# Adding the halves of a narrow expert block on the way out of PSUM, in a decoder trunk with a mixture of experts

## Chip, cores and metric

The kernel runs on 1 core of one Trainium2 chip. The metric is the device time of one execution in microseconds (us); before the change the median of 3 runs is 1606.11 us (1605.93 to 1607.49).

## The reference

A two-layer decoder trunk on 256 tokens of width 1024. What matters here is the last sub-layer, a mixture of 8 SwiGLU experts of which each token takes two, with gates from a softmax over its two logits:

```python
def expert_block(args):
    xb, e = args
    gu = xb @ w13[e]                       # 1024 -> 2 x 3584
    return (jax.nn.silu(gu[:, :EXPERT_DIM]) * gu[:, EXPERT_DIM:]) @ w2[e]
```

Everything is float32. The weights of all eight experts, 8 x 44 MB, are read from HBM once.

## The kernel before

**Precision.** A float32 operand is split in two parts: hi is ScalarE's copy into TensorE's reduced type (L77), lo is what VectorE's subtraction leaves (L78). A product takes three matmuls, hi x hi, hi x lo, lo x hi (`mm3`, L306 to L309).

**Weights.** `Stream` (L35 to L89) loads 1 MB at a time on SyncE's queue (L59) into a handful of raw buffers, and splits each load in two pieces. A split is emitted when the ring `parts` has a free place out of five (N_PARTS, L31), so the split of a piece stands four pieces ahead of its use. A raw buffer is reused when its second piece is subtracted.

**Blocks.** Experts are ordered by their number of tokens ("places" 0 to 7). A wide block holds 128 tokens. A narrow block holds 64, and its gathered input `xs` carries the hi parts in columns 0 to 63 and the lo parts in 64 to 127; so two matmuls with `xs` as the stationary side (L1186, L1187) do the work of three, and the result has the sum split over two halves of partitions: rows 0 to 63 and rows 64 to 127 of PSUM have to be added. Places 0, 2, 3, 4 have a wide block, place 1 a wide and a narrow one, places 5, 6, 7 a narrow one each: four narrow blocks.

**Stages.** An expert is done in slices of 512 of its 3584 hidden columns (j = 0 to 6, L155): stage g (gate projection), stage u (up projection), and, one slice later, stage w (down projection of slice j - 1). A stage takes four pieces. The order of all stages is written out by hand (L163 to L188): places 0, 2, 3 in a chain, then the 21 stages of place 1, each followed by three stages of the chain 7, 6, 5, then place 4. `run_stage` (L1254) projects and takes the result out of PSUM. In stage g a wide block's result goes through Silu on ScalarE (L1297); a narrow block's is copied by ScalarE (L1300). In stage u the wide block's is multiplied in by VectorE (L1303); the narrow block's is copied by ScalarE (L1306), and `hidden` is queued.

**Small steps in between.** `beat_` (L1131), called after each piece, takes one step of the generator at the head of `quick` and, every second time, one of `slow` (gathers, finishing a block). For a narrow block `hidden` (L1189) waits one beat, then in two beats adds the halves of g and of u and transposes them at once, by a matmul of 128 rows of `gs` or `us` against `fold`, two 64 x 64 identities below each other (L1207); Silu (L1209) and the product (L1211) follow on the transposed values, and in a fourth beat the split into hi and lo (L1215, L1216) which stage w takes. A wide block waits three beats, then does four transposes (L1197) and the split.

**Order.** The engines run what is emitted in order. The PSUM pool `mm` has four banks, taken in turn (`bank`, L108).

Of the kernel before, what the change touches and what calls it, by code (L numbers as in the profile page):

```python
# [10 lines left out]
F32 = mybir.dt.float32  # L11
# [3 lines left out]
AF = mybir.ActivationFunctionType  # L15
# [77 lines left out]
def trunk(ctx, tc, x, mem, a_w_in, a_conv_w, a_conv_b, a_w_rgate, a_b_rgate, a_w_igate, a_b_igate,  # L93
# [3 lines left out]
    PE, ACT, DVE, POOL, SP = nc.tensor, nc.scalar, nc.vector, nc.gpsimd, nc.sync  # L97
# [10 lines left out]
    def bank():  # L108
        return psum.tile([128, 512], F32, name="mm")
# [161 lines left out]
    ident = const.tile([128, 128], F32, name="ident")  # L271
# [39 lines left out]
    def w_piece(a_hi, a_lo):  # L311

        p = bank().rearrange("p (m c) -> p m c", m=2)
        for m in range(2):
            w_hi, w_lo = st.get()
            for k in range(KT):
                mm3(p[:, m], w_hi[:, k], w_lo[:, k], a_hi[:, k], a_lo[:, k], k == 0, k == KT - 1)
            if m == 0:
                tick()
        return p  # L320
# [311 lines left out]
    for i in range(4):  # L632
        p = w_piece(x_hi, x_lo)
# [5 lines left out]
    for i in range(2):  # L639
        p = w_piece(x_hi, x_lo)  # L640
# [4 lines left out]
    for i in range(2):  # L645
        p = w_piece(mem_hi, mem_lo)
# [4 lines left out]
    p = t_pieces(mem_hi, mem_lo, 2)  # L651
# [31 lines left out]
    for t in range(2):  # L683
        p = w_piece(mem_hi, mem_lo)
# [45 lines left out]
    p = t_pieces(mem_hi, mem_lo)  # L730
# [161 lines left out]
    for i in range(2):  # L892
        p = w_piece(x_hi, x_lo)
# [3 lines left out]
    for i in range(4):  # L897
        p = w_piece(x_hi, x_lo)
# [4 lines left out]
    for i in range(4):  # L903
        p = w_piece(x_hi, x_lo)
# [6 lines left out]
    for c in range(2):  # L911
        p = t_pieces(x_hi, x_lo)
# [27 lines left out]
    for t in range(2):  # L940
        for h in range(2):
            p = bank().rearrange("p (k c) -> p k c", k=4)
# [13 lines left out]
    mo = ctx.enter_context(tc.tile_pool(name="mo", bufs=1))  # L956
# [3 lines left out]
    def mt():  # L960

        if "mt" not in late:
            assert not any(slot in early for _, slot in st.loaded) and not any(slot in early for slot in st.free)
            ep.close()
            late["mt"] = ctx.enter_context(tc.tile_pool(name="mt", bufs=2))
        return late["mt"]
# [16 lines left out]
    for r in range(2):  # L983
        mr = S(f"m{r}", 2)
        DVE.tensor_reduce(mr, l, axis=AX.X, op=OP.max)
        c = S(f"c{r}", 2, 8)
# [36 lines left out]

    ord_i = mo.tile([1, NE - 1], I32, name="ord_i")
    cs_i = mo.tile([1, NE + 1], I32, name="cs_i")
    fold = mo.tile([128, 64], F32, name="fold")
    y = h3

    h3_parts = []
# [1 line left out]
    def plan():  # L1031

        d = S("d", 2)
        POOL.tensor_sub(d, m[1], m[0])
        ACT.activation(d, d, AF.Exp)
        yield
        cnt = S("cnt", 8)
        DVE.tensor_copy(cnt, ct[:, 16:24])
        POOL.tensor_copy(rank[:, :, 0:1], val[:, :, 0:1])
        q = NE - 1  # L1040
        e7 = slots[:, 1:NE]
        key = S("key", q)
        DVE.scalar_tensor_tensor(key, cnt[:, 1:], 8.0, e7, op0=OP.mult, op1=OP.subtract)
        cmp = S("cmp", q, q)
        DVE.tensor_tensor(cmp, key[:, None, :].to_broadcast([128, q, q]), key[:, :, None].to_broadcast([128, q, q]),
                          op=OP.is_gt)
        yield
        pos = S("pos", q)
        DVE.tensor_reduce(pos, cmp, axis=AX.X, op=OP.add)
        sel = S("sel", q, q)  # L1050
        DVE.tensor_tensor(sel, pos[:, None, :].to_broadcast([128, q, q]),
                          slots[:, 0:q, None].to_broadcast([128, q, q]), op=OP.is_equal)
        yield
        ordr = S("ordr", q)
        POOL.tensor_mul(cmp, sel, e7[:, None, :].to_broadcast([128, q, q]))
        DVE.tensor_reduce(ordr, cmp, axis=AX.X, op=OP.add)
        POOL.tensor_copy(ord_i, ordr[0:1])
        yield
        tmp = S("tmp", 2, q, q)
        for t in range(2):  # L1060
            POOL.tensor_tensor(tmp[:, t], sel, val[:, t, None, 1:].to_broadcast([128, q, q]), op=OP.mult)
        DVE.tensor_reduce(rank[:, :, 1:], tmp, axis=AX.X, op=OP.add)
        yield
        for bs in PLACE.values():
            for b in bs:
                if b[0]:
                    dispatch(b)
            if bs[0][0] % 2:
                yield
        g1 = S("g1", 2)  # L1070
        POOL.tensor_scalar(g1, d, 1.0, None, op0=OP.add)
        DVE.reciprocal(g1, g1)
        POOL.tensor_mul(d, d, g1)
        yield
        ge = S("ge", 2, 8)
        POOL.tensor_tensor(ge, oh[0], bc(g1), op=OP.mult)
        POOL.tensor_tensor(oh[1], oh[1], bc(d), op=OP.mult)
        POOL.tensor_add(ge, ge, oh[1])
        yield
        POOL.tensor_copy(gate[:, :, 0:1], ge[:, :, 0:1])  # L1080
        for t in range(2):
            POOL.tensor_tensor(tmp[:, t], sel, ge[:, t, None, 1:].to_broadcast([128, q, q]), op=OP.mult)
        DVE.tensor_reduce(gate[:, :, 1:], tmp, axis=AX.X, op=OP.add)
        yield
        cs = S("cs", NE)
        POOL.tensor_copy(cs[:, 0:1], cnt[:, 0:1])
        POOL.tensor_mul(cmp, sel, cnt[:, None, 1:].to_broadcast([128, q, q]))
        DVE.tensor_reduce(cs[:, 1:], cmp, axis=AX.X, op=OP.add)
        yield
        room = S("room", NE)  # L1090
        for p in range(NE):
            POOL.memset(room[:, p:p + 1], float(sum(b[2] for b in PLACE[p])))
        POOL.tensor_sub(cs, cs, room)
        over = S("over", 1)
        DVE.tensor_reduce(over, cs, axis=AX.X, op=OP.max)
        yield
        DVE.tensor_scalar(over, over, 0.0, None, op0=OP.max)
        DVE.tensor_scalar(cs, cs, 0.0, None, op0=OP.max)
        POOL.tensor_copy(cs_i[:, :NE], cs[0:1])
        POOL.tensor_copy(cs_i[:, NE:], over[0:1])  # L1100
        yield
        POOL.tensor_add(fold, ident[:, 0:64], ident[:, 64:128])
        h3_parts.extend(hp.tile([128, 2, D], F32R, name=f"h3_{s}") for s in ("hi", "lo"))
        hi, lo = h3_parts
        for t in range(2):
            ACT.activation(hi[:, t], h3[:, t], AF.Copy)
            DVE.tensor_sub(lo[:, t], h3[:, t], hi[:, t].bitcast(F32))
            yield
        for t in range(2):
            ACT.activation(y[:, t], h3[:, t], AF.Copy, scale=ALPHA)  # L1110
            yield
# [65 lines left out]
    def project(o, b, w, kts, w_hi, w_lo, first, last):  # L1177

        for i, kt in enumerate(kts):
            a, z = first and i == 0, last and i == len(kts) - 1  # L1180
            for h in range(len(o)):
# [3 lines left out]
                else:  # L1185
                    PE.matmul(o[h], lhsT=w[:, kt], rhs=w_hi[:, i, f], start=a, stop=False)  # L1186
                    PE.matmul(o[h], lhsT=w[:, kt], rhs=w_lo[:, i, f], start=False, stop=z)  # L1187

    def hidden(b, j):  # L1189

        yield
        if b.wide:
            yield
            yield
            p = bank().rearrange("p (i c) -> p i c", i=4)
            for i in range(4):
                PE.transpose(p[:, i], b.sg[:, i * 128:(i + 1) * 128], ident)  # L1197
            hd = [mt().tile([128, 4, 128], F32R, name="hs", bufs=4) if (b.place, j) == (4, NJ - 1) else
                  mw.tile([128, 4, 128], F32R, name=f"hd_{s}") for s in ("hi", "lo")]
            hi, lo = hd  # L1200
        else:
            h = mt().tile([128, 4, 64], F32, name="sh")
            for src in (b.gs, b.us):

                p = bank()[:, :256].rearrange("p (i c) -> p i c", i=4)
                for i in range(4):
                    PE.matmul(p[:, i], lhsT=src[:, i * 128:(i + 1) * 128], rhs=fold, start=True, stop=True)  # L1207
                if src is b.gs:
                    ACT.activation(h, p, AF.Silu)  # L1209
                else:  # L1210
                    DVE.tensor_mul(h, h, p)  # L1211
                yield
            hd = mt().tile([128, 4, 128], F32R, name="hs", bufs=4)
            hi, lo, p = hd[:, :, 0:64], hd[:, :, 64:], h
        ACT.activation(hi, p, AF.Copy)  # L1215
        DVE.tensor_sub(lo, p, hi.bitcast(F32))  # L1216
        b.h[j] = hd
# [36 lines left out]
    def run_stage(blocks, kind, j, s):  # L1254
# [38 lines left out]
        for b, p in zip(blocks, o):  # L1293
            if kind == "g":
                if b.wide:
                    b.sg = mw.tile([128, 512], F32, name="sg")
                    ACT.activation(b.sg, p, AF.Silu)  # L1297
                else:
                    b.gs = mt().tile([128, 512], F32, name="gs")
                    ACT.activation(b.gs, p, AF.Copy)  # L1300
            else:
                if b.wide:
                    DVE.tensor_mul(b.sg, b.sg, p)  # L1303
                else:
                    b.us = mt().tile([128, 512], F32, name="us")
                    ACT.activation(b.us, p, AF.Copy)  # L1306

                quick.append(hidden(b, j))

    def run_experts(seq, blocks, s, hooks):  # L1310
# [75 lines left out]
    with tc.If(more > 0):  # L1386
        for p in (0, 1, 2, 3, 5, 6, 7):
            c = nc.values_load(cs_i[0:1, p:p + 1], min_val=0, max_val=2 * T,
                               skip_runtime_bounds_check_because="a count of at most 256 tokens")
            with tc.If(c > 0):  # L1390
# [3 lines left out]
                b = Block(key)  # L1394
# [78 lines left out]
```

## Time and profile before

| | |
|---|---|
| median of 3 runs | 1606.11 us (1605.93 to 1607.49) |
| the profiled execution | 1606.54 us |
| its span, first to last instruction | 1604.8 us |
| TensorE's mean granted clock | 0.996 |
| loaded from HBM | 449.00 MB |

The expert layer starts near 557 us. The first narrow stage's result leaves PSUM at 959.4 us (L1300), the last narrow hidden step ends near 1454 us (L1216). How to read the rows: a group gives line, engine, operation, output <- inputs, form, count, then busy us and mean ns of one, then the engine's idle time just before them and what ended it. A time-line row gives the start in us, the length in us, engine, line, operation, output <- inputs, form and count, and in brackets the idle time of the engine before it and what ended that. Matmuls are pipelined, so that their lengths overlap; the time that one holds the engine is the distance between starts.

### The profile page before, as it was taken

To read this page: it belongs to the slowest core of one execution; us is meant where nothing else is said; L and a number is where in the kernel's file an instruction comes from. 1 tells how busy PE (TensorE), PEld (TensorE's weight loads), DVE (VectorE), ACT (ScalarE), POOL (GpSimd) and SP (SyncE) were. 2 spreads that over 40 slices of the span, in tenths; PEclk is the share of its full clock that TensorE was granted. 3 is DMA by queue.
4 is the path that set the end of the run, shared out by engine and by line. 5 is a ranking of instruction groups with operands and counts; after the bars stand their busy time and mean duration, and the time that the engine had idled before them with its cause. 6 is when DMAs were issued, how large, how long until landed. Compare 5 with 4: busy or idle time off the path is not lost.

```text
span 1604.8 us, 23215 instructions
## 1 busy us (share of the span) xinstructions
PE 1582.8 (99%) x8585; PEld 1340.6 (84%) x8585; DVE 1263.1 (79%) x1464; ACT 1091.9 (68%) x1419; POOL 37.1 (2%) x60
## 2 busy tenths in 40 slices
PE   8999999999999999999999999999999999999996
PEld 7988999998998877888888888888888888888775
DVE  6678545546657689888988879888798889789976
ACT  5784544443546368787787778778778777778774
POOL 0000000000000113000000000000000000000000
PEclk9999999999999999999999999999999999999998
DMA  9454655556443789999996999999999999999991
GB/s 290 158 190 151 237 185 185 184 187 205 135 133 135 272 302 352 356 357 332 360 364 224 352 309 341 355 357 370 326 354 359 362 365 345 336 362 359 342 321 47
DMA packets 218682, 451.63 MB, mean 281 GB/s; under 512 B 7241, under 2 KB 62610, under 8 KB 218562
## 3 DMA queue, kind: packets, MB, share of 16 engines
q1 hardware_dynamic: 217490, 446.76, 78.5%
q0 software_dynamic: 1072, 3.32, 0.7%
q8 instruction: 69, 1.13, 0.3%
q14 instruction: 51, 0.42, 0.1%
HBM read 449.00 MB, written 1.05 MB: 280 GB/s over the span
## 4 chain that ended last, share of the span: by engine, by line
PE 93%; DVE 3%; ACT 2%; issue 1%; DMA 1%; POOL 0%; POOLq 0%; SPq 0%; ACTq 0%
PE mm L307 14%; PE mm L309 14%; PE mm L308 14%; PE mm L1186 7%; PE mm L1187 7%; PE acc L307 7%; PE acc L308 7%; PE acc L309 7%; PE mm L1207 3%; PE acc L1186 3%; PE acc L1187 2%; DVE w_lo L78 2%; PE mm L1170 1%; PE mm L1197 1%; ACT w_hi L77 1%
## 5 line engine op out<-in xcount | busy, mean ns | idle before, releaser
L78 DVE TENSOR_TENSOR w_lo<-raw,w_hi 128x1024 fp32r<-128x1024 f32 x509 | 610.1, 1223 | 188.3 <-ACT w_hi L77 184.8
L77 ACT ACTIVATE w_hi<-raw 128x1024 fp32r<-128x1024 f32 x509 | 525.3, 1056 | 141.4 <-PE mm L308 42.8
L307 PE MATMUL mm<-w_hi,xg_hi 128*128 128x512 f32 x560 | 225.2, 402 | 0.2 <-ACT w_hi L77 0.2
L307 PE MATMUL mm<-x_hi,w_hi 128*128 128x256 f32 x768 | 220.4, 287 | 2.4 <-ACT w_hi L77 2.4
L308 PE MATMUL mm<-w_lo,xg_hi 128*128 128x512 f32 x560 | 221.4, 395 | 1.2 <-DVE w_lo L78 1.2
L309 PE MATMUL mm<-w_hi,xg_lo 128*128 128x512 f32 x560 | 221.3, 395 | 0.0
L309 PE MATMUL mm<-x_hi,w_lo 128*128 128x256 f32 x768 | 218.6, 285 | 1.1 <-DVE w_lo L78 1.1
L308 PE MATMUL mm<-x_lo,w_hi 128*128 128x256 f32 x768 | 218.0, 284 | 0.0
L1186 PE MATMUL mm<-w_hi,xs 128*128 128x512 f32 x448 | 179.0, 400 | 0.0
L1187 PE MATMUL mm<-w_lo,xs 128*128 128x512 f32 x448 | 176.9, 395 | 0.0
L307 PEld LDWEIGHTS mm<-x_hi,w_hi 128*128 128x128 f32 x768 | 148.0, 193 | 5.6 <-ACT w_hi L77 2.9
L309 PEld LDWEIGHTS mm<-x_hi,w_lo 128*128 128x128 f32 x768 | 148.0, 193 | 1.7 <-DVE w_lo L78 1.6
L308 PEld LDWEIGHTS mm<-x_lo,w_hi 128*128 128x128 f32 x768 | 148.0, 193 | 0.6
L307 PEld LDWEIGHTS mm<-w_hi,xg_hi 128*128 128x128 f32 x560 | 105.3, 188 | 25.7 <-ACT xs L1352 1.5
L309 PEld LDWEIGHTS mm<-w_hi,xg_lo 128*128 128x128 f32 x560 | 105.1, 188 | 25.2
L308 PEld LDWEIGHTS mm<-w_lo,xg_hi 128*128 128x128 f32 x560 | 105.4, 188 | 24.9 <-DVE w_lo L78 2.2
L78 DVE TENSOR_TENSOR w_lo<-x_hi,w_hi 128x1024 fp32r<-128x1024 f32 x86 | 103.7, 1223 | 15.3 <-ACT w_hi L77 15.2
L78 DVE TENSOR_TENSOR w_lo<-x_lo,w_hi 128x1024 fp32r<-128x1024 f32 x86 | 103.4, 1222 | 13.4 <-ACT w_hi L77 13.2
L78 DVE TENSOR_TENSOR w_lo<-h,w_hi 128x1024 fp32r<-128x1024 f32 x84 | 100.9, 1222 | 14.4 <-ACT w_hi L77 14.0
L307 PE MATMUL acc<-w_hi,hd_hi 128*128 128x512 f32 x272 | 108.1, 398 | 0.0
L308 PE MATMUL acc<-w_lo,hd_hi 128*128 128x512 f32 x272 | 107.4, 395 | 0.0
L309 PE MATMUL acc<-w_hi,hd_lo 128*128 128x512 f32 x272 | 107.4, 395 | 0.0
(379 smaller groups left out, 2645.6 us busy)
## 6 DMA issues: line engine op xcount, KB each, us to landing
raw<-in_moe_w SPq DMA_DIRECT2D x169, 1024.0 KB, 5.5
x_hi<-in_moe_w SPq DMA_DIRECT2D x43, 1024.0 KB, 5.4
x_lo<-in_moe_w SPq DMA_DIRECT2D x43, 1024.0 KB, 6.2
raw<-in_ffn_w SPq DMA_DIRECT2D x42, 1024.0 KB, 5.0
h<-in_moe_w SPq DMA_DIRECT2D x42, 1024.0 KB, 5.5
e<-in_moe_w SPq DMA_DIRECT2D x36, 1024.0 KB, 5.9
raw<-in_a_w_in SPq DMA_DIRECT2D x10, 1024.0 KB, 9.5
raw<-in_mem_w_kv SPq DMA_DIRECT2D x8, 1024.0 KB
```

What stands on the lines that cost most here:

```text
L77: nc.scalar.activation(hi, src, AF.Copy)
L78: nc.vector.tensor_sub(lo, src, hi.bitcast(F32))
L307: PE.matmul(o, lhsT=l_hi, rhs=r_hi, start=start, stop=False)
L308: PE.matmul(o, lhsT=l_hi, rhs=r_lo, start=False, stop=False)
L309: PE.matmul(o, lhsT=l_lo, rhs=r_hi, start=False, stop=stop)
L1170: PE.matmul(p[:, k], lhsT=src[:, t, f], rhs=disp[:, t, g0:g0 + ng], start=t == 0, stop=t == 1)
L1186: PE.matmul(o[h], lhsT=w[:, kt], rhs=w_hi[:, i, f], start=a, stop=False)
L1187: PE.matmul(o[h], lhsT=w[:, kt], rhs=w_lo[:, i, f], start=False, stop=z)
L1197: PE.transpose(p[:, i], b.sg[:, i * 128:(i + 1) * 128], ident)
L1207: PE.matmul(p[:, i], lhsT=src[:, i * 128:(i + 1) * 128], rhs=fold, start=True, stop=True)
```

## The change

The halves are now added as they leave PSUM. ScalarE copies rows 64 to 127 into rows 0 to 63 of an SBUF tile, and VectorE adds rows 0 to 63 from PSUM. In stage g, Silu follows on ScalarE; in stage u, the product on VectorE. `hidden` waits three beats for a narrow block as for a wide one, and transposes the product alone, with four transposes of 64 rows; the split then reads PSUM. The tile `fold` goes.

```diff
-    fold = mo.tile([128, 64], F32, name="fold")
...
-        POOL.tensor_add(fold, ident[:, 0:64], ident[:, 64:128])
...
+    def halves_sum(p, name):
+
+        a = mt().tile([64, 512], F32, name=name)
+        ACT.activation(a, p[64:128], AF.Copy)
+        DVE.tensor_add(a, a, p[0:64])
+        return a
+
     def hidden(b, j):
 
         yield
+        yield
+        yield
+        n, src = (128, b.sg) if b.wide else (64, b.us)
+        p = bank()[:, :4 * n].rearrange("p (i c) -> p i c", i=4)
+        for i in range(4):
+            PE.transpose(p[:, i], src[:, i * 128:(i + 1) * 128], ident[:n, :n])
         if b.wide:
-            yield
-            yield
-            p = bank().rearrange("p (i c) -> p i c", i=4)
-            for i in range(4):
-                PE.transpose(p[:, i], b.sg[:, i * 128:(i + 1) * 128], ident)
...
         else:
-            h = mt().tile([128, 4, 64], F32, name="sh")
-            for src in (b.gs, b.us):
-
-                p = bank()[:, :256].rearrange("p (i c) -> p i c", i=4)
-                for i in range(4):
-                    PE.matmul(p[:, i], lhsT=src[:, i * 128:(i + 1) * 128], rhs=fold, start=True, stop=True)
-                if src is b.gs:
-                    ACT.activation(h, p, AF.Silu)
-                else:
-                    DVE.tensor_mul(h, h, p)
-                yield
             hd = mt().tile([128, 4, 128], F32R, name="hs", bufs=4)
-            hi, lo, p = hd[:, :, 0:64], hd[:, :, 64:], h
+            hi, lo = hd[:, :, 0:64], hd[:, :, 64:]
         ACT.activation(hi, p, AF.Copy)
         DVE.tensor_sub(lo, p, hi.bitcast(F32))
...
                 else:
-                    b.gs = mt().tile([128, 512], F32, name="gs")
-                    ACT.activation(b.gs, p, AF.Copy)
+                    b.gs = halves_sum(p, "gs")
+                    ACT.activation(b.gs, b.gs, AF.Silu)
             else:
...
                 else:
-                    b.us = mt().tile([128, 512], F32, name="us")
-                    ACT.activation(b.us, p, AF.Copy)
-
+                    b.us = halves_sum(p, "us")
+                    DVE.tensor_mul(b.us, b.us, b.gs)
                 quick.append(hidden(b, j))
```

## Rows read from the trace of the kernel before

**Rows 1.** The page, part 1: busy us (share of the span) and instructions.
```profile
PE 1582.8 (99%) x8585; PEld 1340.6 (84%) x8585; DVE 1263.1 (79%) x1464; ACT 1091.9 (68%) x1419; POOL 37.1 (2%) x60
```
**Rows 2.** Windows, 953 to 1453: PE, PEld, DVE, ACT, POOL, clock, DMA share, GB/s.
```profile
953.00:1453.00 500.00, 500.00 (x2440) 413.52 (x2439) 435.37 (x436) 394.14 (x499) 2.09 (x4) 1.00 0.97 351
```
**Rows 3.** Time-line of TensorE, 1051 to 1084.
```profile
1066.35 1.00 PE L1207 MATMUL mm<-fold,gs 128*128 128x64 f32 x8
1067.16 0.48 PE L1186 MATMUL acc<-w_hi,hs 128*128 128x512 f32 x1
...
1073.74 0.40 PE L307 MATMUL mm<-w_hi,xg_hi 128*128 128x512 f32 x1
...
1083.07 0.40 PE L1186 MATMUL mm<-w_hi,xs 128*128 128x512 f32 x1
```
**Rows 4.** Time-line of VectorE, 1060 to 1085.
```profile
1070.50 0.42 DVE L1211 TENSOR_TENSOR sh<-sh,mm 128x256 f32<-128x256 f32 x1
...
1072.35 6.91 DVE L78 TENSOR_TENSOR w_lo<-raw,w_hi 128x1024 fp32r<-128x1024 f32 x6
...
1084.85 1.23 DVE L78 TENSOR_TENSOR w_lo<-h,w_hi 128x1024 fp32r<-128x1024 f32 x1 [1.82 <-ACT w_hi L77]
```
**Rows 5.** Time-line of ScalarE, 1061 to 1086.
```profile
1070.95 0.42 ACT L1215 ACTIVATE hs<-sh 128x256 fp32r<-128x256 f32 x1 [1.05 <-DVE sh L1211]
...
1080.71 1.06 ACT L77 ACTIVATE w_hi<-raw 128x1024 fp32r<-128x1024 f32 x1 [1.27 <-DVE w_lo L78]
...
1083.27 0.60 ACT L1300 ACTIVATE gs<-mm 128x512 f32<-128x512 f32 x1 [0.33 <-PE mm L1187]
```
**Rows 6.** Windows, L1207 alone, 953 to 1453: PE, PEld, clock, DMA share, GB/s.
```profile
953.00:1453.00 500.00, 55.99 (x448) 58.65 (x448) 1.00 0.97 351
```
**Rows 7.** Time-line of TensorE around a wide block's four transposes.
```profile
590.81 0.60 PE L1197 MATMUL mm<-ident,sg 128*128 128x128 f32 x4
591.16 0.48 PE L307 MATMUL mm<-w_hi,xg_hi 128*128 128x512 f32 x1
591.48 0.39 PE L308 MATMUL mm<-w_lo,xg_hi 128*128 128x512 f32 x1
591.71 0.40 PE L309 MATMUL mm<-w_hi,xg_lo 128*128 128x512 f32 x1
```
**Rows 8.** Groups of VectorE, 953 to 1453.
```profile
L78 DVE TENSOR_TENSOR w_lo<-raw,w_hi 128x1024 fp32r<-128x1024 f32 x191 | 226.3, 1222 | 41.4 <-ACT w_hi L77 39.3 <-PE mm L1186 1.8
...
L1211 DVE TENSOR_TENSOR sh<-sh,mm 128x256 f32<-128x256 f32 x28 | 11.7, 416 | 0.0
...
L1281 DVE TENSOR_TENSOR ys<-ys,mm 128x512 f32<-128x512 f32 x12 | 7.7, 681 | 0.0
L1243 DVE TENSOR_TENSOR y_lo<-ys,y_hi 128x512 fp32r<-128x512 f32 x7 | 4.8, 686 | 0.0
```
**Rows 9.** Groups of ScalarE, 953 to 1453.
```profile
L1215 ACT ACTIVATE hs<-sh 128x256 fp32r<-128x256 f32 x28 | 11.7, 418 | 24.9 <-DVE sh L1211 24.9
...
L1242 ACT ACTIVATE y_hi<-ys 128x512 fp32r<-128x512 f32 x7 | 4.4, 622 | 0.0
```
**Rows 10.** Windows, L78 alone, 953 to 1453: DVE, clock, DMA share, GB/s.
```profile
953.00:1453.00 500.00, 394.08 (x335) 1.00 0.97 351
```
**Rows 11.** Time-line of VectorE ahead of two other long stages.
```profile
1116.43 2.44 DVE L78 TENSOR_TENSOR w_lo<-raw,w_hi 128x1024 fp32r<-128x1024 f32 x2
...
1216.51 2.36 DVE L78 TENSOR_TENSOR w_lo<-x_lo,w_hi 128x1024 fp32r<-128x1024 f32 x2
```
**Rows 12.** Time-line of TensorE: first matmul of these two long stages.
```profile
1120.61 0.40 PE L307 MATMUL acc<-w_hi,hd_hi 128*128 128x512 f32 x1
...
1218.51 0.40 PE L307 MATMUL mm<-w_hi,xg_hi 128*128 128x512 f32 x1
```
**Rows 13.** DMA, 953 to 1453: GB/s in 40 equal slices.
```profile
GB/s 258 398 345 317 352 349 380 354 339 354 367 370 386 364 334 346 279 364 321 374 338 361 374 385 367 346 366 345 368 327 335 354 382 353 374 273 390 321 371 353
```

## The prediction

> **What bounds the kernel now.** The page comes first: TensorE is busy 99% of the span, VectorE 79%, ScalarE 68% [rows 1]. That is an average over stages, so the stretch that holds all narrow blocks is read next, 953 to 1453 us [rows 2]: TensorE 500.0 of 500 us, VectorE 435.4, ScalarE 394.1, the DMA engines at 0.97, the granted clock 1.00. The time-line then says how full TensorE really is. One period is a long stage (the wide and the narrow block of place 1 together, four split pieces at 2.33 us) and the three short stages behind it (u, w, g of one narrow block of places 5 to 7). TensorE runs through it without a gap. But the long stage starts at 1073.74 [rows 3], and the subtraction that made its first piece (counted off in the order of use) started at 1072.35 and, at 1.22 us, ended at 1073.57 [rows 4]: 0.17 us to spare. So two engines bound this stretch in turn: TensorE the long stages, in which ScalarE waits 1.27 us for a place in the ring of five pieces and VectorE then 1.82 us for ScalarE [rows 4, 5], and VectorE, just not late, the short ones.
>
> One rule differs here. TensorE's matmuls fill all 500 us, its weight loads 413.5, VectorE 435.4 [rows 2]. The Trainium skill (Perfetto Trace Analysis, Identifying the Most-Contended Engine) says that matmul busy time is a bad measure of headroom and that weight-load share, and occupancy for the other engines, are the good ones. By that rule VectorE would be the bound already and all that is added to it would count, an estimate of 41 to 90 us by the terms below. The trace agrees only in part, since its matmuls follow one another without a gap: the sum lets VectorE's idle time be eaten first.
>
> **What goes from TensorE.** Per narrow block and slice of 512 hidden columns, 28 times: eight fold matmuls, 16 records [rows 6]. Eight records hold the next matmul back from 1066.35 to 1067.16, 0.81 us [rows 3]; behind a group of transposes the first matmul takes 0.32 us to the next start against 0.23 [rows 7], and I charge the folds the same 0.09. So 1.8 us a slice. Four transposes come back. The wide block's four cost 0.35 + 0.09 = 0.44 us [rows 7]; with half the columns perhaps half. I take 0.44, the only row; the other end is 0.2. Net 1.36 us (to 1.6), in all 38 us (to 45) of TensorE time. The fold tile's one addition on GpSimd goes too; that engine is busy 2% [rows 1], and I cost it at nothing; it would still be under a microsecond if nothing covered it.
>
> **What comes to VectorE.** Gone: the product sh out of PSUM, 0.416 us [rows 8]. The subtraction behind it stays, of the same size, now from PSUM. New: two additions of 64 x 512 (SBUF and PSUM) and one product of 64 x 512. No row has 64 partitions. A row's time follows its columns (256: 0.416, 512: 0.681, 1024: 1.222 [rows 8]), so I take the 128 x 512 rows, 0.68 for SBUF with PSUM and 0.69 for SBUF alone; half of that, 0.34, is the low end, and no row speaks for more. In a queue each overlaps its follower by 0.09 (six subtractions take 6.91 us, 1.135 apart [rows 4]). The net is 28 x (3 x 0.60 - 0.33) = 41 us queued, 28 x (3 x 0.68 - 0.416) = 45 us alone, 13 us at the low end.
>
> **What comes to ScalarE.** Two copies and a Silu of 512 columns and a split copy, against two copies, a Silu of 256 and a split copy: some 0.2 us a slice more, 6 us. I cost it at nothing; its cover is the engine's 106 us of idle time [rows 2], and without that it is those 6 us.
>
> **The added wait.** In stage g the Silu stands right behind the copy in ScalarE's order and needs VectorE's addition; the next weight split stands behind the Silu. So VectorE first runs its queue empty up to the addition. Then it has nothing to do until Silu (0.62 for an SBUF-to-SBUF pass of 512 columns [rows 9], 0.1 of it beside its follower) and the next split copy (1.06 [rows 5]) are done. A hop costs 0.03: sh ended at 1070.92, its reader on ScalarE started at 1070.95 [rows 4, 5]. That makes a hole of 0.03 + 0.52 + 1.06 + 0.03, about 1.6 us, in VectorE per slice; 28 are 45 us. ScalarE's present wait for sh, 24.9 us in all [rows 9], goes, but no wait of TensorE hangs on it now, so it gives nothing back. Stage u adds no hole: addition and product stand behind each other on VectorE while ScalarE goes on splitting. SyncE issues a load when a subtraction frees its buffer, so its queue moves with VectorE; no load is moved past another.
>
> **The sum over the stretch.** VectorE needs 435 + 41 (or 45) + 45 = 521 to 525 us. Its lone subtractions close up if it never idles: 394.1 us for 335 [rows 10] is 1.176 each, queued 1.135, 14 us less. So 507 to 525 us against 500: 7 to 25 us longer, while TensorE's own need falls to 462.
>
> **The same, step by step,** for the period at 1073.74. The long stage's four subtractions end at 1072.35 + 3 x 1.135 + 1.22 = 1076.98. Addition, Silu and split copy follow, so the next subtraction starts at 1079.2 instead of 1076.9, and four of them end at 1083.8, 0.7 after the long stage ends (1083.07 [rows 3]).
> After a long g, place 1's narrow half has the same hole: its copy ends at 1083.87 [rows 5], addition, Silu and split copy end near 1086.2, and the next subtraction starts there instead of at 1084.85 [rows 4], 1.35 late. Addition and product (1.2) for one product (0.33) add 0.87; 0.17 was to spare: 2.0 us longer.
> After a long w the two additions into ys stand there as before: 0.75 late, 0.87 more. To spare were 1218.51 less the end of the subtraction begun at 1216.51, 0.78 [rows 11, 12]: 0.85 longer.
> After a long u: 0.7 late, 0.87 more. TensorE had four folds more there, so 1120.61 less the end of the pair begun at 1116.43, 1.74, was to spare [rows 11, 12]: 0.15 shorter.
> Three periods cost 2.7 us, seven rounds 19. Periods that also hold a block's finish or a gather have more to spare and may give back 5. Both ways meet near **16 us**. The profiled execution took 1606.54 us (span 1604.8, 1.7 around it), 0.4 above the median of the runs, so the forecast is 1606 + 16 = **1622 us**.
>
> **Rivals.** (1) TensorE stays the bound and the change is *faster*: 38 us, 1568 us. Place: the hole in stage g. With VectorE's closed-up work at 435 + 41 - 14 = 462 us it decides at (500 - 462) / 28 = 1.36 us a slice; each 0.1 us below that gives 2.8 us. For it: TensorE's 500 of 500, and that an addition on half the partitions, if it took half the time, would take 28 us off the sum, to 1594. Against: nothing can overtake a Silu and a split copy on ScalarE, and the long stage's slack is already spent in the walk. Loads don't cap it: the stretch ran at 351 GB/s [rows 2], with slices of 12.5 us at 398 [rows 13], at which its 175 MB take 441 us. The Trainium skill (Perfetto Trace Analysis, Roofline) gives 358 GB/s as a core's share and about 435 as a lone core's ceiling. By the first only some 10 us could be gained, by the second all 38; the slices above 358 speak for the second. Chance 0.15, from 1568 to 1602.
> (2) Hole and slack cancel, 1606 us: chance 0.08.
> (3) *Much slower*: a PSUM bank was free when ScalarE had copied it; now VectorE's addition frees it, up to three subtractions (3.4 us) later. Four banks rotate, so a bank is wanted again four allocations on. If TensorE waits 1 us for one in each slice, that is 28 us more, 1650 us. Against: four allocations are more than one short stage (3.7 us), and the new hidden step takes one bank where the old one took two. Chance 0.1.
> (4) The change doesn't do what it says: the folds are there, 448 records [rows 6], so this can only be the half-time additions, counted under (1).
>
> **Chances.** VectorE late by work and holes has 0.67; its own range is 1613 to 1631 (7 and 25 us). Within 0.2% (3 us, about what a measurement of this kernel can tell from no change) 0.08; faster 0.15; slower 0.67 + 0.1 = 0.77. To leave out no more than 2 in 10 the range reaches down to 1602, with most of rival 1 outside, and up to 1642, with most of rival 3 outside.
>
> **What would show it.** In the same stretch: VectorE over 92% busy; TensorE with gaps ended by w_lo, at the start of long stages and in the short ones; ScalarE idle ahead of Silu in stage g, ended by VectorE's addition, 28 times 1 to 3 us; VectorE idle some 1.6 us behind that addition, ended by ScalarE's split; additions and products near 0.68 us; transposes near 0.35 us per four. If TensorE has no gap, rival 1 is right and the forecast wrong; if its gaps are ended by a bank's reader, rival 3; if the additions take 0.34 us, the size is wrong.

## The result: slower by 26 us, and the profile after

The median after the change is 1632.67 us (1631.59 to 1634.18, four runs) against 1606.3 for the kernel before in the same session. The ratio is 1.0164, 95% interval 1.0146 to 1.0181. The forecast was 1622 us, range 1602 to 1642, slower with a chance of 0.77. Sign and mechanism came as forecast; the size is 26 us where 16 were forecast. The profiled execution took 1631.59 us, its span is 1629.5, so the two profiled executions differ by 25.05 us.

The page of the kernel after, its busy times (part 1) and the engines of its chain of waits (part 4):

```profile
PE 1578.6 (97%) x8249; PEld 1287.9 (79%) x8249; DVE 1299.6 (80%) x1520; ACT 1102.4 (68%) x1419; POOL 33.3 (2%) x59
...
PE 80%; DVE 12%; ACT 4%; issue 3%; DMA 1%; DVEq 0%; POOLq 0%; POOL 0%; SPq 0%; ACTq 0%
```

Beside [rows 1] TensorE has 336 matmuls fewer (28 slices, each with sixteen records of folds less and four transposes more), and its busy time has hardly fallen. A matmul that waits for its weights may be drawn long (0.50 us for 0.39 in the rows of TensorE below), so busy time hides part of the wait. The chain tells more: of the span, TensorE carries 80% (93% before) and VectorE 12% (3% before).

In what follows *the stretch* runs from the first matmul of place 1 to the first of place 4. It was 949.74 to 1451.64 us before, 501.9 us, and is 949.76 to 1474.31 after, 524.5: 22.6 us of the 25. The windows of the stretch, of before and then of after (columns: PE, PEld, DVE, ACT, POOL, clock, DMA share, GB/s):

```profile
949.00:1452.00 503.00, 503.00 (x2455) 415.98 (x2454) 437.83 (x438) 396.12 (x500) 2.09 (x4) 1.00 0.97 351
```
```profile
949.00:1474.00 525.00, 497.24 (x2114) 362.75 (x2113) 472.10 (x492) 405.43 (x500) 0.64 (x1) 1.00 0.93 335
```

VectorE has 34.3 us more to do and is idle for 52.9 us. The waits of the same stretch of after (engine, what waited, for what; us in all, times, longest):

```profile
ACT gs L1295 <- DVE gs L1191: 82.6, 28, 5.1
DVE w_lo L78 <- ACT w_hi L77: 50.1, 35, 1.6
PEld mm L1185 <- DVE w_lo L78: 36.8, 62, 2.0
PEld acc L1185 <- DVE w_lo L78: 19.4, 45, 1.1
...
PE mm L1185 <- DVE w_lo L78: 13.7, 22, 1.6
...
PE mm L1202 <- DVE us L1301: 5.0, 13, 0.5
...
PE mm L1184 <- DVE h L1227: 1.5, 1, 1.5
```

This is a ring of waits. ScalarE's Silu (L1295) waits 28 times for VectorE's addition, 2.95 us each. VectorE then waits for ScalarE's split, and nearly all of its idle time is that (50.1 of 52.9). TensorE's matmuls and weight loads wait for `w_lo`, and hardly for anything else: no wait for a bank's reader is of any size. One round of it in the time-lines of VectorE, ScalarE and TensorE (a long stage starts at 1081.91):

```profile
1081.32 4.61 DVE L78 TENSOR_TENSOR w_lo<-raw,w_hi 128x1024 fp32r<-128x1024 f32 x4
1085.86 0.67 DVE L1191 TENSOR_TENSOR gs<-gs,mm 64x512 f32<-64x512 f32 x1
1088.18 4.63 DVE L78 TENSOR_TENSOR w_lo<-raw,w_hi 128x1024 fp32r<-128x1024 f32 x4 [1.65 <-ACT w_hi L77]
1092.73 0.67 DVE L1191 TENSOR_TENSOR gs<-gs,mm 64x512 f32<-64x512 f32 x1
1095.05 2.36 DVE L78 TENSOR_TENSOR w_lo<-h,w_hi 128x1024 fp32r<-128x1024 f32 x2 [1.65 <-ACT w_hi L77]
```
```profile
1082.11 0.59 ACT L1190 ACTIVATE gs<-mm 64x512 f32<-64x512 f32 x1
1086.56 0.63 ACT L1295 ACTIVATE gs<-gs 64x512 f32<-64x512 f32 x1 [3.86 <-DVE gs L1191]
1087.10 3.89 ACT L77 ACTIVATE w_hi<-raw 128x1024 fp32r<-128x1024 f32 x4
```
```profile
1081.91 0.39 PE L307 MATMUL mm<-w_hi,xg_hi 128*128 128x512 f32 x1
1082.58 0.50 PE L308 MATMUL mm<-w_lo,xg_hi 128*128 128x512 f32 x1 [0.28 <-DVE w_lo L78]
...
1095.51 0.39 PE L1184 MATMUL acc<-w_hi,hs 128*128 128x512 f32 x1
1096.33 0.50 PE L1185 MATMUL acc<-w_lo,hs 128*128 128x512 f32 x1 [0.42 <-DVE w_lo L78]
```

The copy of the upper half is done at 1082.70, but the addition stands behind four queued subtractions and starts at 1085.86. Silu follows at 1086.56, the split at 1087.10, and the next subtraction at 1088.18: VectorE stood still for 1.65 us, and then again 7 us later. TensorE's next matmul with the lo part comes 0.67 and 0.82 us behind the one ahead of it, where 0.23 is the pace. Compare [rows 3, 4]: TensorE without a gap, and six subtractions one behind the other ahead of the long stage; VectorE's wait of 1.82 us stood within it, where it held nothing up.

The prices of the parts, from VectorE's and ScalarE's groups of after, 953 to 1475:

```profile
L78 DVE TENSOR_TENSOR w_lo<-raw,w_hi 128x1024 fp32r<-128x1024 f32 x189 | 220.9, 1213 | 30.1 <-ACT w_hi L77 29.7
...
L1301 DVE TENSOR_TENSOR us<-us,gs 64x512 f32<-64x512 f32 x28 | 19.1, 683 | 1.0
L1191 DVE TENSOR_TENSOR gs<-gs,mm 64x512 f32<-64x512 f32 x28 | 18.8, 671 | 1.4 <-ACT gs L1190 1.4
L1191 DVE TENSOR_TENSOR us<-us,mm 64x512 f32<-64x512 f32 x28 | 18.8, 671 | 0.0
```
```profile
L1295 ACT ACTIVATE gs<-gs 64x512 f32<-64x512 f32 x28 | 17.7, 632 | 82.6 <-DVE gs L1191 82.6
```

An addition of 64 partitions takes 671 ns, one of 128 took 681 [rows 8]: half the partitions save 10 ns.

Outside the stretch the change costs 0.6 us in the next three stages (the first two of place 4 and the last of place 5, 17.44 to 18.04 us) and 1.5 in *the tail*, taken here from the first matmul of the last stage to VectorE's last instruction: 19.36 us before, 20.85 after. The chain of after shows where, among the eight last matmuls (L1410):

```profile
1612.12 0.70 PE mm L1410
1612.82 1.43 issue
1614.25 3.18 PE mm L1410 x7
```

Before, the same eight took 3.69 us without a break.

### The profile page after: what moved, and what is told of

It is laid out like the page before. It is cut to its first block, busy times and chain, and to the rows that moved or that the text cites. A ratio compares the mean times of both kernels' runs of the same rounds, so it can differ in the third digit from the quotient of the medians.

```text
span 1629.5 us, 22666 instructions
## 1 busy us (share of the span) xinstructions
PE 1578.6 (97%) x8249; PEld 1287.9 (79%) x8249; DVE 1299.6 (80%) x1520; ACT 1102.4 (68%) x1419; POOL 33.3 (2%) x59
## 4 chain that ended last, share of the span: by engine, by line
PE 80%; DVE 12%; ACT 4%; issue 3%; DMA 1%; DVEq 0%; POOLq 0%; POOL 0%; SPq 0%; ACTq 0%
PE mm L308 14%; PE mm L309 13%; PE mm L307 13%; DVE w_lo L78 9%; PE acc L308 7%; PE acc L307 7%; PE acc L309 7%; PE mm L1185 5%; PE mm L1184 5%; ACT w_hi L77 3%; PE mm L1168 1%; PE mm L1202 1%; PE acc L1185 1%; PE acc L1184 1%; DMA raw<-in_a_w_in 0%
## 5 line engine op out<-in xcount | busy, mean ns | idle before, releaser
L78 DVE TENSOR_TENSOR w_lo<-raw,w_hi 128x1024 fp32r<-128x1024 f32 x509 | 606.4, 1218 | 175.6 <-ACT w_hi L77 174.0
L1185 PE MATMUL mm<-w_lo,xs 128*128 128x512 f32 x448 | 183.3, 409 | 13.8 <-DVE w_lo L78 13.7
L1185 PEld LDWEIGHTS mm<-w_lo,xs 128*128 128x128 f32 x448 | 84.0, 187 | 53.6 <-DVE w_lo L78 36.8
L78 DVE TENSOR_TENSOR w_lo<-x_lo,w_hi 128x1024 fp32r<-128x1024 f32 x86 | 102.8, 1216 | 16.4 <-ACT w_hi L77 16.1
L78 DVE TENSOR_TENSOR w_lo<-x_hi,w_hi 128x1024 fp32r<-128x1024 f32 x86 | 102.7, 1216 | 13.2 <-ACT w_hi L77 12.8
L78 DVE TENSOR_TENSOR w_lo<-h,w_hi 128x1024 fp32r<-128x1024 f32 x84 | 99.8, 1215 | 10.6 <-ACT w_hi L77 10.4
```

Of the source, the lines that this page charges most:

```text
L78: nc.vector.tensor_sub(lo, src, hi.bitcast(F32))
```

## The experiments

The theory: VectorE is late because its queue runs empty once a slice, while Silu and the split behind it go round through ScalarE (*the hole*). Rivals: the extra work alone makes it late; TensorE's shorter stages are what exposes it; a longer ring would hide it; or a bank is held. Each result is a median with its lowest and highest time, then its ratio to the kernel before in the same session with a 95% interval. Differences in us are against the kernel after, unless a line says that its kernel is the one before.

### Silu moved behind further splits

Silu becomes a small step of its own, one beat later, so that splits are queued ahead of it. The work is the same.

```diff
-                    ACT.activation(b.gs, b.gs, AF.Silu)
+                    quick.append(silu(b))
...
+    def silu(b):
+        yield
+        ACT.activation(b.gs, b.gs, AF.Silu)
```

> The changed kernel with Silu of a narrow block's g moved one beat and a half back: it is queued as a small step and stands on ScalarE behind two further weight splits, so that ScalarE no longer waits for VectorE's addition ahead of a split. All work of the change stays. Theory (hole behind the addition, 28 x 1.65 us, on a VectorE that is the bound): VectorE then needs about 470 to 485 us in the stretch that took 525, TensorE 462; the stretch takes 475 to 495 and the whole 1583 to 1603 us, below the kernel before. Rival (the additions' work alone made it slower): VectorE's 41 us stay, 1620 to 1633 us. Rival (banks held longer): unchanged, 1630 us or more.

1613.88 us (1611.9 to 1614.54), 1.0039 (1.0025 to 1.0052). That is 18.8 us less than after, but 11 more than the theory's upper end, and the first rival's lower end is 6 higher: neither range holds it. The stretch is 502.4 us, what it was before (501.9). Its windows, then VectorE's time-line in the place of the round shown above:

```profile
949.00:1451.00 502.00, 484.87 (x2110) 365.73 (x2107) 473.02 (x491) 406.49 (x498) 0.64 (x1) 1.00 0.98 349
```
```profile
1079.61 0.67 DVE L1191 TENSOR_TENSOR gs<-gs,mm 64x512 f32<-64x512 f32 x1
1080.20 3.48 DVE L78 TENSOR_TENSOR w_lo<-raw,w_hi 128x1024 fp32r<-128x1024 f32 x3
1084.31 1.23 DVE L78 TENSOR_TENSOR w_lo<-raw,w_hi 128x1024 fp32r<-128x1024 f32 x1 [0.62 <-ACT w_hi L77]
```

The same additions and products, 473.0 us of VectorE's time against 472.1, and the subtraction follows the addition at once. So, with the work in place, the hole costs the 22 us of the stretch. The work without the hole still eats, with a ring of five, the 38 us that TensorE was relieved of: the stretch is no shorter than before. What is left over the kernel before is the tail: 25.14 us here against 19.36, 5.8 of the 7.3 us between the profiled executions. TensorE's time-line there:

```profile
1592.34 2.05 PE L1415 MATMUL mm<-gs,sh 128*128 128x512 f32 x2 [3.90 <-PEq L1385]
```

TensorE stands still 3.90 us, put down to its own sequencer at L1385, the branch around a part of the program that is not run here. Then the eight matmuls take 6.38 us. The windows of the gap and of these eight:

```profile
1588.00:1592.30 4.30, 0.44 (x2) 0.00 (x0) 0.69 (x1) 0.60 (x1) 0.00 (x0) 0.84 0.01 4
1592.30:1599.00 6.70, 6.36 (x8) 2.47 (x8) 2.51 (x4) 0.00 (x0) 0.00 (x0) 0.59 0.00 0
```

The granted clock is 0.59 after the gap, near the lower level (1.2 of 2.4 GHz); before the change, with no such gap, it was 1.00, and after the gap of 1.43 us in the kernel after it was 1.00 too. The DMA view of the gap has one packet in it, of the instruction queue:

```profile
q8 instruction: 1, 0.02, 1.4%
```

TensorE waits for code, it seems. The Trainium skill (Runtime: NRT & Kernel Launch, Instruction fetch mechanics) says that a taken branch to a page of code that is not at hand stalls the engine until it is fetched. The trace agrees as far as it goes, with 3.9 us at the branch and a packet in them. In the kernel after it agrees less well: the 1.43 us stand between the first and the second of the eight matmuls, and the packet (1611.97 to 1612.91) ends as they begin.

### The code behind the branch moved

The kernel with the later Silu, and nine spare warm-up matmuls in each of the seven bodies that are jumped over. None of them runs; the code behind them only lies elsewhere.

```diff
+                keep_warm(9)
```

> The changed kernel with Silu moved back, and nine matmuls in each of the seven bodies of the overflow branch, which is not taken: nothing more is executed, but TensorE's instructions behind the branch lie elsewhere. Theory (the eight last matmuls came 4.3 us late, 1587.8 to 1592.3, and then ran at a clock of 0.59, because TensorE had no instructions behind the branch): the stretch stays at 502 us and the time falls by 2 to 6 us, 1608 to 1612 us, if the new place is a better one. Rival (the late tail comes from the moved Silu): 1613 to 1615 us.

1608.3 us (1607.6 to 1610.41), 1.0012 (1.0002 to 1.0022), with a stretch of 503.8 and a tail of 19.26. The first of TensorE's eight last matmuls:

```profile
1592.82 1.13 PE L1416 MATMUL mm<-gs,sh 128*128 128x512 f32 x2 [0.69 <-ACT gs L1410]
```

The gap is gone, and the time-line shows the eight in 3.7 us. So moving code that is not run removes it, and the tail is no part of the change's design; the lesson of the stretch stands without it. That TensorE waited for code is likely, not shown: the gap is also absent with a ring of six or seven places, where no code was moved on purpose, and it comes again (3.48 us) in the last kernel below, with a ring of five.

### The hole alone, in the kernel before

Behind the copy of g one column makes the round through VectorE and ScalarE; nothing else differs from before.

```diff
                     ACT.activation(b.gs, p, AF.Copy)
+                    DVE.tensor_copy(b.gs[:, 0:1], b.gs[:, 0:1])
+                    ACT.activation(b.gs[:, 0:1], b.gs[:, 0:1], AF.Copy)
```

> The kernel before, with the wait alone: behind the copy of a narrow g out of PSUM, VectorE rewrites one column of it and ScalarE rewrites that column again, so ScalarE waits for VectorE ahead of its next split just as in the changed kernel, without the additions' work and with the folds in place. Theory (hole and work share VectorE's idle time, 65 us in this stretch, and cost only what goes beyond it): 28 holes of some 1.4 us and 28 x 0.1 us fit, 2 to 8 us slower, 1608 to 1614 us. Rival (a hole costs its length wherever it stands): 28 x 1.4 = 39 us, 1645 us.

1609.22 us (1607.73 to 1609.87), 1.0011 (1.0002 to 1.002). ScalarE's wait, and VectorE's hole in the time-line:

```profile
ACT gs L1302 <- DVE gs L1301: 30.2, 28, 2.8
```
```profile
1078.45 0.14 DVE L1301 COPY gs<-gs 128x1 f32<-128x1 f32 x1
1079.81 4.76 DVE L78 TENSOR_TENSOR w_lo<-raw,w_hi 128x1024 fp32r<-128x1024 f32 x4 [1.22 <-ACT w_hi L77]
```

28 holes of 1.22 us (shorter than 1.65, for one column passes ScalarE faster), 34 us in all, cost 2.5 us. VectorE had 65 us of idle time in this stretch and has room for them. So neither these holes nor the work (the experiment with the later Silu) makes the stretch more than 2 us longer than before by itself; in the change each takes the room that the other needs. The test is not quite of the same size: the changed kernel's holes are 46 us.

### TensorE's folds put back

Each narrow slice of the kernel after does eight spare fold matmuls, in two beats of `hidden`, whose result nobody reads.

```diff
+                PE.matmul(p[:, i], lhsT=ident, rhs=fold, start=True, stop=True)
```

> The changed kernel with eight spare fold matmuls per narrow hidden step on constant data, into a PSUM bank that nobody reads: TensorE's work of the kernel before comes back, 28 x 1.8 = 50 us, in the beats where it stood. Theory (VectorE sets the stretch, TensorE has 63 us of room in it): 0 to 12 us slower, 1633 to 1645 us. Rival (TensorE's own work still sets a good part of the time): 50 us slower, 1683 us.

1637.54 us (1637.31 to 1639.02), 1.0192 (1.0176 to 1.0207): 4.9 us more than after. The group of the folds, of the same size as [rows 6]:

```profile
L1201 PE MATMUL mm<-fold,ident 128*128 128x64 f32 x448 | 55.9, 268 | 0.0
```

56 us of TensorE's records cost 4.9 us (in the trace 8.2 in the stretch, and the tail, without the break, is 1.6 shorter). The 38 us that went from TensorE were therefore worth little here, since TensorE was waiting for `w_lo` anyway.

### A ring of six pieces

Three kernels exchange a raw buffer for a sixth place in the ring: with the later Silu, the kernel before, and the kernel after.

```diff
-N_RAW = 4
-N_PARTS = 5
+N_RAW = 3
+N_PARTS = 6
```

> The changed kernel with Silu moved back (as in the first experiment) and the ring of split pieces six places long instead of five, paid for by one raw buffer less (three instead of four of them). Theory (with the hole gone, VectorE is late in the short stages only because the ring keeps it from working ahead in the long stages): the stretch of the narrow blocks, 502.4 us with Silu moved back alone, falls towards VectorE's and TensorE's need of 465 to 485, at least 8 us less, and VectorE's idle time in it below 20 us. Rival (loads set it, or the raw buffer is missed): 502 us or more.

1592.89 us (1591.87 to 1593.97), 0.9912 (0.9896 to 0.9929), faster than both kernels. The stretch is 491.4 us, 11 less than with five places; its windows:

```profile
947.00:1439.00 492.00, 480.22 (x2117) 374.31 (x2115) 472.34 (x492) 403.67 (x500) 0.64 (x1) 0.99 0.98 357
```

VectorE is idle for 19.7 us, against 29 with five.

> The kernel before with six places in the ring and three raw buffers instead of five and four. Theory (TensorE, at 500 of 500 us with the folds, sets the stretch before the change): within 3 us of the kernel before, 1604 to 1610 us, or slower if the raw buffer is missed. Rival (the ring's length held the kernel before back as well): faster by 5 us or more.

1604.18 us (1603.72 to 1605.94), 0.9985 (0.9975 to 0.9994), and the stretch is 501.9 us as before: where TensorE is full, the ring gives nothing. So the 11 us above come from the later Silu and the longer ring together. With the same ring of six, the changed kernel with the later Silu is 11 us faster than the kernel before.

> The changed kernel as it is, with Silu behind the addition, and six places in the ring with three raw buffers. Theory (the hole is VectorE's own time, since the next subtraction waits for a split that stands behind Silu, whatever stock there is): the 28 holes of 1.65 us stay, VectorE needs 470 + 46 = 516 us, and the stretch takes 505 to 520 us, 1612 to 1627 in all. Rival (a longer ring hides the hole): as with Silu moved back and six places, 1593 to 1600 us.

1627.43 us (1626.52 to 1628.18), 1.013 (1.0114 to 1.0145). The stretch is 524.7 us, not shortened at all; the 5 us come from outside it (3.7 between the two profiled executions: 1.5 ahead of the experts, 0.5 behind the stretch and 1.6 from a tail without the break). ScalarE's wait and the hole are as they were:

```profile
ACT gs L1295 <- DVE gs L1191: 88.6, 28, 5.3
```
```profile
1091.30 0.67 DVE L1191 TENSOR_TENSOR gs<-gs,mm 64x512 f32<-64x512 f32 x1
1093.62 3.50 DVE L78 TENSOR_TENSOR w_lo<-raw,w_hi 128x1024 fp32r<-128x1024 f32 x3 [1.65 <-ACT w_hi L77]
```

All 28 holes have this length. A longer ring does not hide them: the splits that would fill it stand behind Silu on ScalarE.

### A ring of seven

The later Silu with two raw buffers and seven places.

> Silu moved back, seven places in the ring and two raw buffers. Theory (with six places VectorE is busy 466 of 486 us, so little is left to gain): 1587 to 1594 us. Rival (loads, with two raw buffers fewer than at first, come late): slower than with six places, 1597 us or more, with ScalarE's splits waiting for loads.

1606.34 us (1598.44 to 1607.76), 0.9992 (0.9981 to 1.0002): the theory missed, and the rival came. The stretch goes on falling, to 487.0 us, but place 1 starts at 962.30 us, 14.6 later than with six. That is lost at the start of the program, long before the experts: TensorE's same matmul comes 15.4 us later at 165 us already. Up to 170 us, ScalarE's splits wait 30.2 us for loads with two raw buffers, and 15.8 with three.

### The product on GpSimd

In the kernel after, the product of stage u goes to GpSimd, which is busy 2%.

```diff
-                    DVE.tensor_mul(b.us, b.us, b.gs)
+                    POOL.tensor_mul(b.us, b.us, b.gs)
```

> The changed kernel with the product of g and u on GpSimd in place of VectorE; the wait in stage g stays. Theory (VectorE's time sets the stretch one for one): 28 x 0.6 to 0.68 = 17 to 19 us less, 1612 to 1618 us, with holes of 1.65 us as before. Rival (the wait alone sets it, not VectorE's work): within 4 us of the changed kernel, 1629 to 1637 us.

1722.54 us (1719.3 to 1730.13), 1.0711 (1.0694 to 1.0727): both expectations wrong by far. GpSimd's group and the waits:

```profile
L1301 POOL TENSOR_TENSOR us<-us,gs 64x512 f32<-64x512 f32 x28 | 129.9, 4640 | 817.7 <-DVE us L1191 804.1 <-PE acc L1185 7.1 <-PE acc L1184 6.5
```
```profile
PEld mm L1202 <- POOL us L1301: 95.8, 19, 5.7
...
PE mm L1202 <- POOL us L1301: 87.6, 19, 5.3
```

The product takes 4.64 us on GpSimd and 0.68 on VectorE, and the transposes, queued ahead of TensorE's next matmuls, wait for it. To see whether the waiting or the operation is to blame, a last kernel with the later Silu lets GpSimd multiply `gs` by itself, behind VectorE's product; no reader of the result follows.

```diff
                     DVE.tensor_mul(b.us, b.us, b.gs)
+                    POOL.tensor_mul(b.gs, b.gs, b.gs)
```

> Silu moved back, ring of five, and a spare product of 64 x 512 on GpSimd behind VectorE's product in each slice, over the tile of g that is dead by then; nobody reads it. Theory (GpSimd's product was slow in itself beside VectorE's and ScalarE's traffic): its 28 runs have a median of 3 to 6 us and some over 7, TensorE isn't held up, and the time stays within 1610 to 1618 us. Rival (it was slow only by what it waited for): all near the shortest seen, 1.29 us.

1622.84 us, one run. GpSimd's group:

```profile
L1307 POOL TENSOR_TENSOR gs<-gs 64x512 f32<-64x512 f32 x28 | 236.9, 8461 | 603.6 <-DVE us L1306 560.3 <-ACT w_hi L77 34.2 <-ACT y_hi L1242 9.1
```

8.46 us on the mean (a median of 7.7, above the theory's 3 to 6), and single ones from 1.87 to 14.48: the product is long beside this VectorE load, whoever waits for it. The stretch is 511.1 us, 8.7 more than without the product; ScalarE's next copy into the tile waits for it 6 times, 23.1 us in all, which no one had counted on. The Trainium skill (SBUF — State Buffer, Who interferes with whom) says that a VectorE instruction with two SBUF inputs and a GpSimd one that reads SBUF exclude each other, the later one waiting. Every split's subtraction has two SBUF inputs, and the trace agrees. One of the long products, and VectorE near its end (at 1087.37):

```profile
1073.22 14.15 POOL L1307 TENSOR_TENSOR gs<-gs 64x512 f32<-64x512 f32 x1 [8.52 <-DVE us L1306]
```
```profile
1082.99 3.48 DVE L78 TENSOR_TENSOR w_lo<-raw,w_hi 128x1024 fp32r<-128x1024 f32 x3
1087.10 1.35 DVE L78 TENSOR_TENSOR w_lo<-raw,w_hi 128x1024 fp32r<-128x1024 f32 x1 [0.63 <-ACT w_hi L77]
```

The product ends 0.90 us after a subtraction (1086.47) behind which VectorE stood idle. All 28 end so, 0.90 us after a subtraction that is followed by idle time or by an instruction that reads PSUM (not every such break ends one: some instructions of 0.4 us on PSUM pass within a product). The 150 subtractions that ran wholly within a product took 1.21 us as elsewhere; only those that run across its end are longer (1.34 to 1.72), which brings the mean to 1228 ns from 1212. The earlier kernel with GpSimd's product shows the other order: seven products began just ahead of a subtraction and took 1.29 us, and that subtraction took 2.2 to 2.4 us instead of 1.21. So nearly all of the 8.46 us is waiting for a break in VectorE's stream; the work in it, by these figures, is some 0.9 to 1.3 us.

## Why the prediction was right in sign and short in size

**What goes from TensorE** was rightly left out of the gain. Some 38 us went, as estimated (four transposes of 64 rows hold the next matmul back by 0.36 to 0.39 us, no less than the wide block's 0.35), and putting the folds back costs 4.9.

**What comes to VectorE**: 671, 671 and 683 ns, as taken from the 128-partition rows. The low end of 0.34 us for half the partitions is excluded, and with it the 1594 us of rival 1.

**What comes to ScalarE**: its busy time in the stretch rose by 9.3 us, where 6 were estimated. That this costs nothing was not tested by itself.

**The added wait**: 1.65 us a hole where 1.6 were forecast, with the forecast's chain of addition, Silu, split, subtraction. That it decides is shown: moving Silu alone takes back the whole 22 us of the stretch. Two signs came only nearly: VectorE is busy 90% of the stretch where over 92% was named, and ScalarE's waits ahead of Silu, 2.95 us on the mean, reach 5.1 where 1 to 3 were named.

**The sum over the stretch** gave VectorE a need of 507 to 525 us in a stretch of 500, 7 to 25 us more, and nearly the upper end came: 22.6, from 501.9 to 524.5. Its lower end rested on the lone subtractions closing up by 14 us. They closed up by 6: L78 alone is busy 387.97 us for 335 in the stretch of after, 1.158 each, against 396.69 for 337 before, 1.177. Behind each hole a subtraction starts alone again, which the lower end left out. The holes and the smaller waits made 52.9 us of idle time where 45 were forecast. These are two of the mis-sized terms.

**Step by step** the third shows. From the start of one long stage to the next, the stretch has 21 periods, eleven of them plain (no block's finish, no gather, not at an end). After a long g these grew from 22.32 to 24.46 us, 2.14 each (three; forecast 2.0). After a long w, from 22.32, they grew by 0.34 to 1.68, in three of five by 1.01 (forecast 0.85). After a long u they grew from 24.55 to 25.00, 0.45 (three; forecast 0.15 *shorter*). The eleven make 12.8 us; the forecast's figures make 9.8 for them. The ten others hold a block's finish or a gather, or stand at the ends, and by the forecast they were to add only 4 (19 less 5 less 9.8). They added 9.85: six grew by 1.3 to 2.6, one stayed, three shrank by 0.4 to 1.0. So of the 8.6 us that the stretch lies above this way's 14, 3.0 come from plain periods that were priced too low and 5.6 from "may give back 5", which failed. The trace of before shows why. Counted off as the prediction did it, nine of the ten (all but the last) had 9.8 us to spare at their ends, and as many plain ones of the same kinds would have had 8.5: 1.4 us more, not 5. The middle of both ways, 16, rested on that and on the 14 us of closing up.

**Outside the stretch** the forecast had nothing. The stages just behind it took 0.6 us, and the break behind the branch 1.5.

**Rivals.** Rival 1 put its deciding point in the hole, and the runs confirm the place: with the hole gone the kernel still stands at 502.4, not at 462, since the ring of five leaves VectorE idle for 29 us, and six places give 11 of it back. So "VectorE's idle time be eaten first" was too simple: idle time in one period is not to be had in another when only a few pieces can be made ahead. Nor does all that comes to VectorE count, priced at 41 to 90 us: 26 came. Rival 2 is excluded by the interval. Rival 3 is excluded by the waits: TensorE's are for `w_lo`. Rival 4 fell with the additions' length.

## What to carry to other kernels

When work moves from a full engine to one that is idle on the average, look at the queues and not only at the busy shares: a step that goes to another engine and comes back, queued ahead of the work that feeds the receiver, empties its queue once per turn, and here a longer ring did not mend that. Queue the return step behind some of the feeding work (here Silu as a step of its own, 18.8 us), and count the slack period by period. Only then did a longer ring pay: together they beat the kernel before by 0.9%.

## What the runs showed of the hardware

- VectorE's 64 x 512 addition takes 671 ns where the 128 x 512 one takes 681 [rows 8]: half the partitions save next to nothing.
- GpSimd's 64 x 512 product takes 1.3 to 14.5 us beside VectorE's stream of subtractions, against 0.68 on VectorE. In the last kernel all 28 ended 0.90 us after a subtraction with a break behind it, and the subtractions within them were no longer than elsewhere (1.21 us); a product that began first took 1.29 us, and the subtraction behind it 2.2 to 2.4.
- Behind a branch over code that is not run, TensorE stood still for 1.4, 3.5 or 3.9 us in three kernels and not in the others; in one, moving code that is not run removed the 3.9. After 3.9 us the next eight matmuls ran at a granted clock of 0.59, in 6.38 us where they take 3.7.
